# Pads between the memory pools of a two-block transformer kernel: moving operands 256 instead of 192 bytes behind the weights

## The chip, the cores and the metric

The kernel runs on 1 core of one Trainium2 chip. The metric is the device time of one execution in microseconds; three runs of the kernel before gave a median of 2269.2 us (2267.66 to 2282.68). Engines are named as in the profile: PE is TensorE's matmuls, PEld its weight loads, DVE is VectorE, ACT is ScalarE, POOL is GpSimd, SP is SyncE.

## What is computed

Two transformer stacks, one after the other, on 256 tokens of width 1024, all in float32:

```python
def first_block(x, ...):
    for i in range(DEPTH):                       # 4 layers
        m, j = i % N_MIXERS, i // N_MIXERS
        h = rms_norm(x, attn_norm[i])
        if m == 0:
            mix = diff_attention(h, a_w_qkv[j], ...)
        elif m == 1:
            mix = latent_attention(h, b_w_a[j], ...)
        else:
            mix = dilated_attention(h, c_w_qkv[j], ...)
        x = x + mix
        x = x + swiglu(rms_norm(x, ffn_norm[i]), f_w_gu[i], f_w_out[i])
    return rms_norm(x, final_norm)

def second_block(x, positions, ...):
    h = layer_norm(x, ln_in_g, ln_in_b)
    for l in range(DEPTH_2):                     # 2 layers
        mix = token_mix(h, ...)                  # pooling, causal convolution, sparse attention, gates
        h = layer_norm(DEEPNORM_ALPHA * h + mix, ln1_g[l], ln1_b[l])
        ffn = conv_ffn(h, w_up[l], ffn_dw_w[l], ffn_dw_b[l], w_down[l])
        h = layer_norm(DEEPNORM_ALPHA * h + ffn, ln2_g[l], ln2_b[l])
    return h
```

Nearly all the work is in projections of the form activations times weight matrix, with 256 tokens.

## The kernel before

**Three products for one.** Every float32 operand of a projection is split into a high and a low part of the type that TensorE takes at its fast rate (R, float32r). `weights` (L300) brings a weight tile from HBM into a tile "raw", ScalarE writes the high part "whi", VectorE or GpSimd the low part "wlo" (L313). `mm3` (L292) then issues three matmuls: whi with the high part of the activations, whi with the low part, wlo with the high part. All three lie on one line of the profile, L270 (`matmul`), and they are told apart there by their tiles.

**Two ways to project.** In `smode` and `smode2` (L330, L336) a 128x128 piece of the weights is the stationary operand and 256 tokens of activations are the moving operand. This is the form of the feed-forward layers (`ffn` L531, `conv_ffn` L1676), of `down` and of the output projections. In `mmode` (L353) a 128x128 piece of the activations is stationary and up to 512 columns of weights move; this is the form of the attention projections.

**Where operands lie.** Activations are either in the token block (tiles xh and xl, L388, 8 rows of 384 columns each) or in tiles "s" of the pool "big" (L262, four rows of 256 columns). Weights are in the pool "w" (raw, whi, wlo, tiles of up to 1024 columns, 4,096 bytes). The pools "const", "w", "big" and "wk" are laid out one behind the other in each partition's memory. Between them stand four tiles that nothing reads or writes, the pads: "padx" before xh, "padw" before the pool w, "padb" before big, "padk" before wk. Their widths in float32 columns are the tuple PADS (L32):

```python
PADS = (56, 72, 48, 80)
...
            pad = lambda n, cols: pool(n, 1).tile([128, cols], F32, name=n)
            pad("padw", PADS[1])
            self.wp = pool("w", 3)
            pad("padb", PADS[2])
            self.big = pool("big", 12)
            pad("padk", PADS[3])
            self.wk = pool("wk", 2)
```

In the built program all row lengths, tile sizes and steps of 128 weight columns of the large projections are multiples of 512 bytes, so the place of each operand, taken modulo 512, is the same for every row and tile of its pool: whi and wlo start at byte 75,968 and 100,544 (192 of 512), xh and xl at 25,472 and 37,760 (384), the tiles of big at 125,312 and multiples of 512 behind it (384). So in `smode` the moving operand lies 384 - 192 = 192 bytes of each 512 behind the weights, and in `mmode`, with the roles exchanged, 192 - 384 = 320 of 512. Two other places matter below: in `stacked_scores` (L650) stationary and moving operand both come from big, at a distance of 0 of 512; and the taps of the convolution (L1635) move `taps[:, n, d:d + 256]`, whose start goes up by 4 bytes with each tap d, high part (n = 0) from 384 of 512, low part (n = 1) 1,144 bytes behind it.

**Order.** TensorE's instructions stand in the order in which the program issues them, with a matmul's weight load ahead of it. Attention steps are woven into the projections by estimated times (`tick`, `later`), with a table of a matmul's duration by its columns (US, L29). Neither depends on the pads.

Of the kernel before, what the change touches and what calls it, by code (L numbers as in the profile page):

```python
# [28 lines left out]
US = {256: 0.12, 288: 0.132, 328: 0.155, 384: 0.175, 512: 0.235}  # L29
POOLED = (5, 7)  # L30
NH = 18
PADS = (56, 72, 48, 80)  # L32
WARM = 10
NORM, POOL = (7, 8, 9), 8
FILL = -3.0e38
# [177 lines left out]
class Program:  # L213
    def __init__(self, tc, ins, out, at):
# [3 lines left out]
        with ExitStack() as ctx:  # L218
            pool = lambda n, b, **k: ctx.enter_context(tc.tile_pool(name=n, bufs=b, **k))
            self.const = pool("const", 1)  # L220
# [7 lines that stand above are left out]
# [143 lines left out]
    def setup(self):  # L371
# [14 lines left out]
        self.ident = self.col("ident", 0, 128)  # L386
        c.tile([128, PADS[0]], F32, name="padx")
        self.xh = c.tile([128, 8, 384], R, name="xh")  # L388
# [1350 lines left out]
```

## Time and profile before

| | us |
|---|---|
| median of 3 runs | 2269.2 (2267.66 to 2282.68) |
| the profiled execution, its own time | 2279.07 |
| its span, first to last instruction | 2277.3 |
| TensorE matmuls busy | 2200.4 (97%) |
| VectorE busy | 1624.8 (71%) |
| ScalarE busy | 1325.4 (58%) |
| mean granted TensorE clock | 0.981 of full |

Matmul records overlap, since matmuls are pipelined: the record of one begins when it starts to read and its end is modelled. So the time that one costs in a dense stretch is the step from its start to the start of the next. In a table of stretches this comes out as the length of the stretch, plus the part of a record that hangs over, divided by the count.

### The profile page before, as it was taken

What the parts mean: (1) busy time and instruction counts of PE and PEld (TensorE: products, weight loads), DVE (VectorE), ACT (ScalarE), POOL (GpSimd) and SP (SyncE); (2) the same over time, 40 slices, a digit from 0 to 9 for tenths busy, and PEclk for the clock granted to TensorE, in tenths of its full rate; (3) what the DMA queues carried; (4) which work ended last, traced back from release to release, by engine and by line L of the source; (5) the groups of instructions that cost most, each with busy time, mean ns of one, the idle gap of its engine ahead of it and who ended that gap; (6) DMA issues with size and microseconds to landing.
All of it is one profiled execution on the core that took longest, in us unless ns stands there. A gap on an engine that the chain in (4) does not pass through costs nothing.

```text
span 2277.3 us, 42526 instructions
## 1 busy us (share of the span) xinstructions
PE 2200.4 (97%) x16676; PEld 2077.3 (91%) x16676; DVE 1624.8 (71%) x2940; ACT 1325.4 (58%) x2378; POOL 147.4 (6%) x169
## 2 busy tenths in 40 slices
PE   9999998999999999999999999989989998998998
PEld 7899997899978778999978999889989998998998
DVE  7776666776556656766577766796888789778875
ACT  7764457544556655644587545645567564656653
POOL 0000000100000000000000001110012011001211
PEclk9999999999999999999999999999989999998999
DMA  6345563355654334455633655544536544443653
GB/s 233 132 155 187 159 186 121 116 195 158 186 198 144 111 132 137 140 186 160 214 122 109 216 174 162 180 151 138 178 119 215 162 160 156 162 163 124 213 160 109
DMA packets 111801, 365.69 MB, mean 161 GB/s; under 512 B 12528, under 2 KB 14704, under 8 KB 111600
## 3 DMA queue, kind: packets, MB, share of 16 engines
q1 hardware_dynamic: 109728, 360.17, 48.1%
q10 hardware_dynamic: 1728, 2.54, 0.4%
q8 instruction: 131, 2.15, 0.4%
q14 instruction: 70, 0.57, 0.1%
q0 software_dynamic: 144, 0.26, 0.1%
HBM read 362.13 MB, written 1.05 MB: 159 GB/s over the span
## 4 chain that ended last, share of the span: by engine, by line
PE 72%; DVE 7%; ACT 4%; issue 1%; POOL 0%; ACTq 0%; DVEq 0%; POOLq 0%
PE mm L270 62%; PE sc L270 6%; PE tp L324 3%; DVE wlo L313 1%; ACT whi L241 1%; PE tp L270 1%; ACT xh L241 1%; ACT s L241 1%; ACT x L241 1%; PE tp L1141 0%; DVE score L1487 0%; DVE mx L1486 0%; PE tp L734 0%; DVE gut L244 0%; DVE acc L1130 0%
## 5 line engine op out<-in xcount | busy, mean ns | idle before, releaser
L313 DVE TENSOR_TENSOR wlo<-raw,whi 128x1024 fp32r<-128x1024 f32 (+3 forms) x752 | 844.7, 1127 | 337.4 <-ACT whi L241 334.0
L241 ACT ACTIVATE whi<-raw 128x1024 fp32r<-128x1024 f32 (+3 forms) x752 | 731.4, 978 | 559.8 <-PE mm L270 343.4
L270 PE MATMUL mm<-xh,wlo 128*128 128x256 f32 x2496 | 703.7, 282 | 16.7 <-DVE wlo L313 16.7
L270 PE MATMUL mm<-xh,whi 128*128 128x256 f32 x2496 | 710.3, 285 | 1.3 <-ACT whi L241 0.9
L270 PE MATMUL mm<-xl,whi 128*128 128x256 f32 x2496 | 703.6, 282 | 0.5 <-DVE xl L1191 0.5
L270 PE MATMUL mm<-s,whi 128*128 128x256 f32 x2944 | 524.4, 281 | 0.2 <-DVE s L244 0.2
L270 PEld LDWEIGHTS mm<-xh,wlo 128*128 128x128 f32 x2496 | 478.8, 192 | 17.6 <-DVE wlo L313 17.6
L270 PEld LDWEIGHTS mm<-xh,whi 128*128 128x128 f32 x2496 | 473.5, 190 | 3.8 <-ACT whi L241 1.3
L270 PEld LDWEIGHTS mm<-xl,whi 128*128 128x128 f32 x2496 | 475.1, 190 | 1.6 <-DVE xl L1191 0.9
L270 PEld LDWEIGHTS mm<-s,whi 128*128 128x128 f32 x2944 | 450.7, 188 | 2.6 <-issue 1.1
L270 PE MATMUL mm<-s,wlo 128*128 128x256 f32 x1472 | 412.3, 280 | 0.0
L270 PEld LDWEIGHTS mm<-s,wlo 128*128 128x128 f32 x1472 | 279.6, 190 | 0.0
L270 PE MATMUL mm<-whi,xh 128*128 128x512 f32 (+2 forms) x592 | 238.5, 404 | 8.2 <-ACT whi L241 4.4
L270 PE MATMUL mm<-wlo,xh 128*128 128x512 f32 (+2 forms) x592 | 233.2, 394 | 3.5 <-DVE wlo L313 3.5
L270 PE MATMUL mm<-whi,xl 128*128 128x512 f32 (+2 forms) x592 | 232.4, 393 | 0.0
L270 PEld LDWEIGHTS mm<-whi,xh 128*128 128x128 f32 x592 | 113.4, 192 | 29.9 <-ACT whi L241 5.0
L270 PEld LDWEIGHTS mm<-wlo,xh 128*128 128x128 f32 x592 | 113.7, 192 | 23.4 <-DVE wlo L313 4.8
L270 PEld LDWEIGHTS mm<-whi,xl 128*128 128x128 f32 x592 | 113.5, 192 | 22.0
L241 ACT ACTIVATE s<-guh 128x256 fp32r<-128x256 f32 x132 | 54.7, 415 | 103.8 <-DVE guh L558 93.3
L510 POOL TENSOR_TENSOR rstd<-ms,nhalf 128x2 f32<-128x2 f32 x29 | 30.0, 1034 | 1061.9 <-DVE ms L508 1053.5
L554 DVE TENSOR_TENSOR gut<-mm,rbc 128x512 f32<-128x512 f32 x88 | 60.4, 690 | 37.4 <-PE mm L270 37.2
L244 DVE SCALAR_TENSOR_TENSOR gut<-mm,pk,gut 128x255 f32<-128x255 f32 (+1 forms) x160 | 76.2, 478 | 7.2 <-ACT gut L241 5.0
(327 smaller groups left out, 2509.8 us busy)
## 6 DMA issues: line engine op xcount, KB each, us to landing
raw<-w_gu SPq DMA_DIRECT2D x176, 512.0 KB, 4.2
raw<-w_up SPq DMA_DIRECT2D x88, 512.0 KB, 4.3
raw<-w_zs SPq DMA_DIRECT2D x60, 512.0 KB, 4.7
raw<-w_out SPq DMA_DIRECT2D x64, 384.0 KB, 3.5
raw<-w_cqk SPq DMA_DIRECT2D x48, 512.0 KB, 4.2
raw<-w_out SPq DMA_DIRECT2D x64, 320.0 KB, 2.9
raw<-w_aqk SPq DMA_DIRECT2D x32, 512.0 KB, 4.8
raw<-w_cv SPq DMA_DIRECT2D x24, 512.0 KB, 3.6
```

The source lines that it names most:

```text
L241: return self.nc.scalar.activation(out, in_, func, bias=bias, scale=scale, **kw)
L244: return self.nc.vector.scalar_tensor_tensor(out, a, s, b, op0=op0, op1=op1)
L270: i = self.nc.tensor.matmul(*a, **kw)
L313: e.tensor_sub(lo, raw, hi.bitcast(F32))
L324: i = self.nc.tensor.transpose(out, in_, self.ident if ident is None else ident)
L510: self.powered = [self.nc.gpsimd.tensor_tensor(r, ms, self.nhalf[:, :n], op=OP.pow).ins]
L554: nc.vector.tensor_mul(t, ps, rb[:, None, :].to_broadcast([128, 2, 256]))
```

## The change

The widths of the four pads are set otherwise. Nothing else is changed.

```diff
-PADS = (56, 72, 48, 80)
+PADS = (72, 56, 64, 80)
```

"padx" grows by 16 columns (64 bytes) and "padw" shrinks by as much, so xh and xl move up by 64 bytes and the weights stay where they are. "padb" grows by 64 bytes, so big moves up by 64 bytes, and wk behind it too. In the built program:

| operand | byte before | of 512 | byte after | of 512 |
|---|---|---|---|---|
| xh | 25,472 | 384 | 25,536 | 448 |
| whi | 75,968 | 192 | 75,968 | 192 |
| tiles of big | 125,312 | 384 | 125,376 | 448 |
| first tile of wk | 174,784 | 192 | 174,848 | 256 |

So the moving operand of `smode` lies 448 - 192 = 256 bytes of each 512 behind the weights, and in `mmode` it is 192 - 448 = 256 of 512 as well. `stacked_scores` stays at 0. On every engine the same instructions stand in the same order as before, with the same waits.

## Rows read from the trace of the kernel before

**Rows 1.** The page: busy time by engine, and the chain's shares by line.

```profile
PE 2200.4 (97%) x16676; PEld 2077.3 (91%) x16676; DVE 1624.8 (71%) x2940; ACT 1325.4 (58%) x2378; POOL 147.4 (6%) x169
...
PE mm L270 62%; PE sc L270 6%; PE tp L324 3%; DVE wlo L313 1%; ACT whi L241 1%; PE tp L270 1%; ACT xh L241 1%; ACT s L241 1%; ACT x L241 1%; PE tp L1141 0%; DVE score L1487 0%; DVE mx L1486 0%; PE tp L734 0%; DVE gut L244 0%; DVE acc L1130 0%
```

**Rows 2.** Groups by form, PE: line, tiles, shape, count, busy us, mean ns, idle.

```profile
L270 PE MATMUL mm<-xh,whi 128*128 128x256 f32 x2464 | 700.3, 285 | 0.9 <-ACT whi L241 0.9
...
L270 PE MATMUL mm<-s,whi 128*128 128x256 f32 x2944 | 524.4, 281 | 0.2 <-DVE s L244 0.2
L270 PE MATMUL mm<-s,wlo 128*128 128x256 f32 x1472 | 412.3, 280 | 0.0
L270 PE MATMUL mm<-whi,xh 128*128 128x512 f32 x544 | 222.8, 411 | 8.2 <-ACT whi L241 4.4 <-ACT s L241 2.5 <-ACT qtok L241 1.1
```

**Rows 3.** Stretches: us, busy us (count) of PE, PEld, DVE, ACT, POOL, clock, DMA, GB/s.

```profile
152.00:302.00 150.00, 150.00 (x1276) 150.00 (x1275) 98.82 (x134) 72.91 (x109) 0.00 (x0) 1.00 0.56 177
449.00:599.00 150.00, 150.00 (x1276) 150.00 (x1276) 98.50 (x131) 72.25 (x106) 1.79 (x3) 1.00 0.59 187
949.00:1099.00 150.00, 150.00 (x1276) 150.00 (x1276) 98.89 (x134) 73.00 (x109) 0.00 (x0) 1.00 0.58 182
1262.00:1402.00 140.00, 140.00 (x1191) 140.00 (x1190) 92.58 (x124) 70.96 (x107) 2.75 (x3) 1.00 0.58 184
1409.00:1436.00 27.00, 27.00 (x232) 27.00 (x231) 25.06 (x37) 17.72 (x32) 9.60 (x10) 1.00 0.62 209
1696.00:1816.00 120.00, 120.00 (x1061) 120.00 (x1060) 98.03 (x154) 75.71 (x122) 17.84 (x15) 1.00 0.60 195
1822.00:1850.00 28.00, 28.00 (x240) 28.00 (x239) 25.07 (x39) 17.30 (x30) 6.77 (x7) 1.00 0.64 211
2006.00:2043.00 37.00, 37.00 (x328) 37.00 (x327) 30.46 (x62) 21.05 (x33) 0.00 (x0) 1.00 0.42 144
2105.00:2225.00 120.00, 120.00 (x1021) 120.00 (x1020) 94.96 (x147) 73.39 (x120) 19.09 (x15) 1.00 0.58 188
2236.00:2263.00 27.00, 27.00 (x241) 27.00 (x240) 17.00 (x28) 10.06 (x17) 6.27 (x7) 1.00 0.26 83
```

**Rows 4.** Groups by line in 152 to 302 us, then 1,696 to 1,816 us.

```profile
L270 PE MATMUL mm<-xh,wlo 128*128 128x256 f32 x314 | 88.2, 281 | 0.0
...
L270 PEld LDWEIGHTS mm<-xh,wlo 128*128 128x128 f32 x313 | 60.1, 192 | 0.0
L270 PEld LDWEIGHTS mm<-xl,whi 128*128 128x128 f32 x313 | 58.8, 188 | 0.0
...
L270 PE MATMUL mm<-xh,wlo 128*128 128x256 f32 x277 | 76.5, 276 | 0.0
...
L270 PEld LDWEIGHTS mm<-xh,wlo 128*128 128x128 f32 x276 | 51.8, 188 | 0.0
```

**Rows 5.** Timeline at 61.5 us (start, us, engine), then the loads' mean in ns.

```profile
61.78 1.60 PE L270 MATMUL sc<-s,s 128*128 128x256 f32 x12
...
L270 PEld LDWEIGHTS sc<-s,s 128*128 128x128 f32 x12 | 1.6, 191 | 0.1
```

**Rows 6.** Timeline of PE, taps 1, 11 and 13, and the matmul after tap 15.

```profile
1533.55 0.40 PE L270 MATMUL sc<-s,whi 128*128 128x256 f32 x2
...
1537.15 0.40 PE L270 MATMUL sc<-s,whi 128*128 128x256 f32 x2
...
1538.85 0.40 PE L270 MATMUL sc<-s,whi 128*128 128x256 f32 x2
...
1539.92 0.28 PE L270 MATMUL mm<-xh,whi 128*128 128x256 f32 x1
```

**Rows 7.** Timeline of PE in the first layer's query and key projection.

```profile
72.17 0.39 PE L270 MATMUL mm<-whi,xl 128*128 128x512 f32 x1
...
73.54 0.39 PE L270 MATMUL mm<-whi,xl 128*128 128x512 f32 x1
```

## Prediction, made before the result

> **What bounds the kernel now.** I read the page first (busy time and the chain that ended last), then the groups by line and form, then stretches by time, and last single rows of TensorE. TensorE is busy 97% of the span, and 62% of the chain is the one line that issues matmuls into the "mm" banks [rows 1]. So the end is set by how densely the matmuls follow each other, and nothing else in the change touches that: every engine keeps its instructions and their order, only addresses differ.
>
> Most of this work has one shape: 128x128 weights, 256 moving columns. There are three products for each pair, so 3 x 2,464 with the token block as moving operand (xh, xl), and 2,944 + 1,472 with tiles of the big pool ("s"): 11,808 matmuls [rows 2]. Their records are about 280 ns long but overlap; what counts is the step from one start to the next. In ten stretches the table shows TensorE filled without a hole, at the full clock (1.00, the level of 2.4 GHz), so the step is the window plus one record, over the count. In 152 to 302 us it is (150.00 + 0.28)/1,276 = 117.8 ns, and the same in two further stretches of that length; in 1,696 to 1,816 us it is (120.00 + 0.28)/1,061 = 113.4 ns [rows 3]. By this the ten stretches fall into two levels and nothing between: seven at 117 to 118 ns (1,276 + 1,276 + 1,276 + 1,191 + 232 + 240 + 1,021 = 6,512 matmuls in 765 us) and three at 113 to 114 ns (1,061 + 328 + 241 = 1,630 in 184 us). Both levels hold for hundreds of matmuls, with the same shapes, the same clock and the same 192 bytes of distance.
>
> The rows of one stretch of each kind show where they differ. At the upper level a matmul's record is 281 ns, and of the three weight loads of a triple one takes 192 ns and two take 188; at the lower level the records are 276 ns and every load takes 188 [rows 4]. So at the upper level a weight load is held up by something that recurs with the triple. VectorE and ScalarE do not explain it: they are busier in the lower-level stretch (98.03 and 75.71 of 120 us) than in the upper one (98.82 and 72.91 of 150 us) [rows 3]. What recurs with the triple is what TensorE itself reads: moving columns of one matmul while the next weights are loaded.
>
> The trace of before also has a few matmuls at other distances, since some operands lie differently. In the score products of the first layer weights and moving operand both come from the big pool, so their distance is 0 of 512. Twelve of them follow each other in (1.60 - 0.28)/11 = 120.0 ns, with loads of 191 ns on average: nearly every load is held up [rows 5]. And the taps of the convolution slide their moving operand by 4 bytes per tap (high part 192 + 4d bytes behind the weights, low part 312 + 4d). From tap 1 to tap 11 (196 to 236 bytes) 30 matmuls take 3.60 us, 120.0 ns each; in taps 13 to 15 (244 to 252 bytes) nine take 1.07 us, 118.9 ns each [rows 6].
>
> **The change part by part.** It removes and adds nothing. Moving operands in the token block and the big pool move up by 64 bytes, weights stay, so 192 becomes 256. Where the roles are exchanged (token block as weights, 512 weight columns moving) the distance goes from 320 to 256. The work pool moves by 64 bytes too, which leaves its distance to the big pool at 192 and touches only transposes and small products; I set those at nothing.
>
> The first term is the step of the 256-column matmuls at 256 bytes. No stretch of before has it with aligned rows, so it is bounded from both sides by the nearest rows. Below: the lower level, 113.4 ns, everywhere. The seven long stretches then give back 6,512 x (117.8 - 113.4) = 29 us. The matmuls outside the ten stretches are 11,808 - 8,142 = 3,666; with the same share of upper-level steps they would give another 13 us, so 42 us in all. Above: 120.0 ns everywhere, as at distance 0. The ten stretches hold 8,142 matmuls in 949 us; at 120.0 they take 977 us, 28 us more, and the others add 28 x 3,666/8,142 = 13 us: 41 us more.
>
> Between these ends I take the gain of the long stretches alone, 29 us, and nothing for the rest, because there the matmuls stand in short groups between other work. What leans to this side: 256 is the distance farthest from 0 both ways round, and 0 is where the rows show a load held up each time; and the taps get shorter, not longer, as they come near 256. It is a weak lean: the taps lie off the alignment of the big matmuls, their low part is elsewhere again, and 1.1 ns x 11,808 is only 13 us.
>
> The Trainium skill, page "TensorE: Matmul & The Clock Gate", section "Part 2: What happens when you issue a matmul", says that TensorE has two independent read ports, so that loading the next weights takes no read bandwidth from the running matmul. By that rule distance would do nothing and the sum would be 0; the 191 ns loads at distance 0 speak against it, the two levels at one distance for it [rows 4, 5].
>
> The second term is the 512-column matmuls, 3 x 544 [rows 2]. Their step is (73.54 - 72.17)/6 = 228 ns [rows 7], 7% over twice 106.7 ns, the 256 columns' own time at 2.4 GHz. With 3 ns either way, as between the levels above, 1,632 of them make 5 us up or down; I take 0.
>
> What hides a gain: nothing in the long gate and up stretches, where VectorE is busy two thirds to four fifths of the time and DMA 0.56 to 0.60 [rows 3]. In the stretch at 1,409 us VectorE has 25.06 of 27 us; at the lower level that work would fill it to 96%, so those 232 matmuls may keep a microsecond of their step. What is late next everywhere else is still TensorE.
>
> Sum: -29 us. The profiled execution took 2279.1 us (span 2277.3), which would become 2250; the three timed runs have a median of 2269.2 and reach from 2267.7 to 2282.7. The profiled one is thus near their upper end, which two long stretches at the other level would explain (1,276 x 4.4 ns = 5.6 us each). I set the sum against the median: 2240 us.
>
> **The rivals.**
> One, distance is not what decides, or 192 and 256 are alike. The level is then drawn anew after each stall: with all long stretches at the lower level it is 29 us less, with all at the upper one 1,630 x 4.4 ns = 7 us more, and as likely as not about the same number of each, so 2269 us. For it: both levels stand at one distance, and it changes from one stretch to another. Against it: distance 0 has a third, longer step.
>
> Two, it becomes slower: distance counts only within a shorter period than 512, of 128 or 256 bytes, because a weight load reads several parts of its 512 bytes side by side. Then 256 is the same as 0, each load is held up from the first matmul on, and no stretch reaches the lower level. The price is the upper end above, 28 to 41 us; I take 35, so 2304 us. It decides as soon as the parts are 256 bytes or shorter. For it: the step of 120.0 ns and the held-up loads at distance 0. Against it: the taps at 244 to 252 bytes don't get longer, though none of them lies exactly at 256 with aligned rows.
> The Trainium skill, same page, section "Weight-path perf modes", describes a weight load in four parallel chunks of 32 columns for types other than FP32; with 4 bytes per column that would be parts of 128 bytes, and the sum would be that of this rival. The trace cannot say whether it applies to these loads.
>
> **How the numbers follow.** A measurement here tells about 1% (23 us) from no change. Forecast 0.38, first rival 0.31, second rival 0.31. The forecast lies over the line of 1%, most of the first rival within it, the second over it on the other side. So faster 0.38, same 0.31, slower 0.31. The forecast's own range is 2225 (42 us, and a little) to 2252. The whole range has to reach over the other cases: from 2222 to 2308, with the far ends of either mechanism left out.
>
> **What would show it.** In the stretch from 152 us on, 150 us would hold 1,326 matmuls at the lower level, 1,276 if nothing changes, 1,252 at 120 ns. Right: records of 276 ns and loads of 188 in all gate and up stretches, no load group at 192. Wrong by the first rival: again stretches of both kinds, perhaps others than now. Wrong by the second: all loads at 191 to 192, and no stretch under 120 ns. A step under 113 ns, or over 120, would mean that neither of my bounds holds.

## The result, and the profile after

The changed kernel takes 2300.8 us (median; single runs 2298.8 to 2302.7), the kernel before 2268.4 us on the same chip (2267.3 to 2282.7): the ratio is 1.0132, with a 95% interval from 1.0105 to 1.0158. It became slower, by 32 us. The prediction of 2240 us was wrong in its sign; the measured time lies within its whole range, close to the second rival's 2304 us.

The page's line of busy times, of the changed kernel (that of before: [rows 1]):

```profile
PE 2227.5 (97%) x16676; PEld 2108.2 (92%) x16676; DVE 1626.9 (71%) x2940; ACT 1324.9 (58%) x2378; POOL 150.5 (7%) x169
```

Only TensorE's two rows have grown by more than 3 us (27 and 31); VectorE, ScalarE and GpSimd do the same work in nearly the same time. The stretches of [rows 3], after the change (columns as there: us, busy us and count of PE, PEld, DVE, ACT and POOL, granted clock, DMA share, GB/s):

```profile
152.00:302.00 150.00, 150.00 (x1252) 150.00 (x1251) 96.86 (x131) 71.06 (x108) 0.00 (x0) 1.00 0.54 173
...
1262.00:1402.00 140.00, 140.00 (x1170) 140.00 (x1170) 94.91 (x125) 68.45 (x101) 2.29 (x2) 1.00 0.57 186
...
1696.00:1816.00 120.00, 116.77 (x959) 116.36 (x958) 99.69 (x161) 77.92 (x133) 23.31 (x18) 0.99 0.53 176
1822.00:1850.00 28.00, 28.00 (x233) 27.85 (x232) 20.21 (x35) 13.24 (x22) 3.58 (x4) 1.00 0.46 140
```

The first shows 1,252 matmuls where before it was 1,276: (150.00 + 0.28)/1,252 = 120.0 ns. The two levels of before (117.8 and 113.4 ns) are both gone. (Later windows no longer begin at the same place of the program, since the work in front of them takes longer; the third has a gap at its start, the fourth the end of the stretch.) The groups by line in 152 to 302 us, to be held against the first half of [rows 4]:

```profile
L270 PE MATMUL mm<-xh,wlo 128*128 128x256 f32 x312 | 88.3, 283 | 0.0
...
L270 PEld LDWEIGHTS mm<-xh,whi 128*128 128x128 f32 x311 | 59.7, 192 | 0.0
L270 PEld LDWEIGHTS mm<-xl,whi 128*128 128x128 f32 x311 | 59.7, 192 | 0.0
L270 PEld LDWEIGHTS mm<-xh,wlo 128*128 128x128 f32 x311 | 59.7, 192 | 0.0
```

Now every one of the three loads of a triple takes 192 ns, where before one took 192 and two 188. The groups by form, against [rows 2]:

```profile
L270 PE MATMUL mm<-xh,whi 128*128 128x256 f32 x2464 | 707.1, 287 | 0.2
...
L270 PE MATMUL mm<-s,whi 128*128 128x256 f32 x2944 | 538.2, 284 | 0.0
L270 PE MATMUL mm<-s,wlo 128*128 128x256 f32 x1472 | 416.9, 283 | 0.0
L270 PE MATMUL mm<-whi,xh 128*128 128x512 f32 x544 | 221.0, 407 | 8.0 <-ACT whi L241 4.2 <-ACT s L241 2.5 <-ACT qtok L241 1.1
```

Where the time came from: I took, of all 256-column matmuls of the two groups, the differences of consecutive starts that are 130 ns or less (11,491 of them before, 11,505 after), and from here on a "step" is such a difference. Its mean goes from 116.8 to 119.9 ns; over 11,808 matmuls that is 37 us more. The same for the 512-column matmuls gives 229.8 before and 228.4 ns after, 2 us less over 1,632. That is 35 us more, where the profiled spans differ by 23.5 (2277.3 and 2300.8). Most of what lies between is the granted clock: its mean in the profiled execution is 0.981 before and 0.987 after, so by an estimate before lost 0.019 x 2277 = 43 us of full-speed time and after 0.013 x 2301 = 30 us. That the pads moved the clock is not shown: timed executions of the kernel before have means from 0.981 to 0.988. The timed medians are 32 us apart, near the 35.

### The profile page after: what moved, and what is told of

Its sections match the earlier page's. It is cut to its first block, busy times and chain, and to the rows that moved or that the text cites. A ratio compares the mean times of both kernels' runs of the same rounds, so it can differ in the third digit from the quotient of the medians.

```text
span 2300.8 us, 42526 instructions
## 1 busy us (share of the span) xinstructions
PE 2227.5 (97%) x16676; PEld 2108.2 (92%) x16676; DVE 1626.9 (71%) x2940; ACT 1324.9 (58%) x2378; POOL 150.5 (7%) x169
## 4 chain that ended last, share of the span: by engine, by line
PE 73%; DVE 6%; ACT 4%; issue 1%; POOL 0%; ACTq 0%; DVEq 0%; POOLq 0%
PE mm L270 63%; PE sc L270 6%; PE tp L324 2%; DVE wlo L313 1%; ACT whi L241 1%; PE tp L270 1%; ACT xh L241 1%; ACT x L241 1%; ACT s L241 0%; DVE score L1487 0%; PE tp L1141 0%; PE tp L734 0%; DVE mx L1486 0%; DVE gut L244 0%; DVE acc L1130 0%
## 5 line engine op out<-in xcount | busy, mean ns | idle before, releaser
L270 PE MATMUL mm<-s,whi 128*128 128x256 f32 x2944 | 538.2, 284 | 0.0
L270 PEld LDWEIGHTS mm<-xh,whi 128*128 128x128 f32 x2496 | 482.6, 193 | 2.6 <-issue 1.0
L270 PEld LDWEIGHTS mm<-xl,whi 128*128 128x128 f32 x2496 | 482.8, 193 | 1.5 <-DVE xl L1191 0.9
L270 PEld LDWEIGHTS mm<-s,whi 128*128 128x128 f32 x2944 | 460.4, 192 | 2.1 <-issue 1.1
L270 PEld LDWEIGHTS mm<-wlo,xh 128*128 128x128 f32 x592 | 113.3, 191 | 22.6 <-DVE wlo L313 4.8
```

The costliest lines, as they stand in the source:

```text
L270: i = self.nc.tensor.matmul(*a, **kw)
```

## The experiments

In all kernels of the first seven runs only the four pads differ, so every engine has the same instructions in the same order. Two distances can be set apart: that of the token block to the weights (7,392 matmuls of 256 columns) and that of the big pool's tiles (4,416). My theories: (P) the distance counts with a period of 128 bytes (distances that differ by 128 act alike), (H) with a period of 256, (W) with a period of 512 and 256 a bad value in it, (A) not the distance counts but the place of the moving block. Each kernel's ratio is to the kernel before, timed on the same chip. The two windows shown of each run lie in the gate and up groups of the first layer (160 to 250 us, token block) and in its down projection (275 to 315 us, big pool). Before, they hold 767 and 342 matmuls, 117.7 and 117.8 ns each:

```profile
160.00:250.00 90.00, 90.00 (x767) 90.00 (x766) 62.39 (x82) 43.54 (x64) 0.00 (x0) 1.00 0.55 181
275.00:315.00 40.00, 40.00 (x342) 40.00 (x341) 23.13 (x32) 18.36 (x27) 0.00 (x0) 1.00 0.61 180
```

**Distance or place.** The weights come down to 128 of 512, the moving blocks stay at 384.

```diff
-PADS = (56, 72, 48, 80)
+PADS = (56, 56, 64, 80)
```

> The pads (56, 56, 64, 80): the moving blocks of both groups of products stay at 384 of 512 bytes, where they lay before the change, and the weights come down to 128 of 512 in their place, so that the distance is 256, as after the change. If the distance decides (by either period), the kernel is as after the change: every long stretch at 120.0 ns, 1,252 matmuls in a window of 150 us, 2295 to 2305 us. If the place of the moving block in 512 bytes decides, it is as before the change: stretches at about 113.4 and 117.8 ns, 1,270 matmuls or more in such a window, 2262 to 2285 us.

2303.0 us, ratio 1.0150 (1.0112 to 1.0188).

```profile
160.00:250.00 90.00, 90.00 (x752) 90.00 (x751) 61.08 (x80) 43.02 (x64) 0.00 (x0) 1.00 0.56 176
275.00:315.00 40.00, 40.00 (x336) 40.00 (x335) 23.15 (x33) 18.26 (x26) 0.00 (x0) 1.00 0.64 181
```

(90 + 0.28)/752 and (40 + 0.28)/336 are 120.0 and 119.9 ns. The moving operands lie where they lay before, and the kernel is as after the change, where it was the weights that kept their place: what the two have in common is the distance. (A) falls.

**One part alone.** Only the token block goes to 256.

```diff
-PADS = (56, 72, 48, 80)
+PADS = (72, 56, 48, 80)
```

> The pads (72, 56, 48, 80): only the token block's moving operands (7,392 of the 11,808 matmuls of 256 columns of the two groups) lie 256 behind their weights, the other 4,416 stay at 192. If the distance sets each matmul's step by itself, the token block's stretches stand at 120.0 ns and the others at 113.4 or 117.8 ns; the time is between: 7,392 x 3.2 ns = 24 us over the kernel before, 2285 to 2298 us. If a stretch's level is drawn once for the whole run and the distance only shifts the draw, both groups move together: all at 120.0 (about 2300 us) or none (about 2269 us).

2283.6 us, ratio 1.0060 (1.0040 to 1.0079), a little under the expected band.

```profile
160.00:250.00 90.00, 90.00 (x752) 90.00 (x751) 61.04 (x80) 43.19 (x64) 0.00 (x0) 1.00 0.55 176
275.00:315.00 40.00, 40.00 (x355) 40.00 (x354) 23.11 (x34) 19.29 (x28) 0.00 (x0) 1.00 0.67 188
```

The token block stands at 120.0 ns: the distance acts on each group by itself. But the other group, whose distance of 192 was not touched, went from 117.8 to 40.28/355 = 113.5 ns. Over the run 86% of its steps are now 113 or 114 ns, where it was 26% before. That gives back (116.6 - 114.0) x 4,416 = 11 us of the 3.0 x 7,392 = 22 us that the token block loses. This was not expected by any theory; the last runs go after it.

**64 and 128.**

```diff
-PADS = (56, 72, 48, 80)
+PADS = (40, 104, 32, 80)
```

> The pads (40, 104, 32, 80): token block at a distance of 64, the other group at 128. If the period is 128 bytes, 64 is as 192 (steps of 113.4 or 117.8 ns) and 128 is as 256 (120.0 ns): 4,416 x 3.2 ns = 14 us over the kernel before, 2275 to 2290 us. If the period is 256 bytes and only 0 of it is bad, both are fast: 2260 to 2285 us with no stretch at 120.0. If it is 512 bytes with 256 alone special, nothing forbids a third level at either distance.

2275.9 us, ratio 1.0038 (1.0017 to 1.0058): within the bands of both periods. The traces tell them apart: at 64 the two levels of before, at 128 no level at all, only 45% of the steps at 119 to 121 ns (table below). (P) falls.

```profile
160.00:250.00 90.00, 90.00 (x767) 90.00 (x766) 62.39 (x82) 43.56 (x64) 0.00 (x0) 1.00 0.57 181
275.00:315.00 40.00, 40.00 (x339) 40.00 (x338) 22.89 (x33) 18.56 (x27) 0.00 (x0) 1.00 0.63 177
```

In the second window a matmul at 128 takes 40.28/339 = 118.8 ns.

**224 and 160.**

```diff
-PADS = (56, 72, 48, 80)
+PADS = (56, 64, 40, 80)
```

> The pads (56, 64, 40, 80): token block at a distance of 224, the other group at 160, neither a multiple of 64. If what counts is how far the distance is from a multiple of 128, both lie between the good 192 and the bad 256 or 128, and the steps lie between 113.4 and 120.0 ns: 2265 to 2290 us. If what counts is that the two are not multiples of 64 bytes, so that no draw between two levels is left, both groups stand at one level: 113.4 ns throughout would be 11,808 x (116.8 - 113.4) = 40 us under the kernel before, 2225 to 2240 us; 117.8 throughout would be 12 us over it, 2275 to 2285 us.

2290.0 us, ratio 1.0087 (1.0053 to 1.0122), the upper end of the first band. Neither group has a level; the means are 118.3 (token) and 117.8 ns. That no level is left off the multiples of 64 held; that both groups would then stand at one step throughout did not.

**320 and 0.**

```diff
-PADS = (56, 72, 48, 80)
+PADS = (72, 40, 0, 80)
```

> The pads (72, 40, 0, 80): token block at a distance of 320, the other group at 0. So far 256 gave 120.0 ns at nearly every step, 64 and 192 two levels (113.4 and 117.8 ns), 128 scattered steps with a mean of 118.6 to 119.0. If the rule has a period of 256 bytes, 320 is as 64 (two levels) and 0 is as 256 (120.0 ns): the group at 0 then costs 4,435 x 3.2 ns = 14 us over the kernel before, 2275 to 2292 us. If 256 alone of the 512 bytes is special (the far end), 0 is another value than 120.0: either a longer step, if the load and the moving block then meet in the same bank at the same time (130 ns or more would be 60 us over), or a shorter one (113.4 throughout: 15 us under, 2255 us).

2296.1 us, ratio 1.0115 (1.0072 to 1.0159), 4 us above the band of the period of 256. Its windows:

```profile
160.00:250.00 90.00, 90.00 (x766) 90.00 (x766) 62.23 (x81) 43.55 (x64) 0.00 (x0) 1.00 0.56 180
275.00:315.00 40.00, 40.00 (x336) 40.00 (x335) 22.72 (x32) 17.86 (x25) 0.00 (x0) 1.00 0.61 178
```

Distance 0 is 40.28/336 = 119.9 ns, the same as 256. What I had left out is the 512-column matmuls, which with the roles exchanged lie at 192 here: 233.3 ns against 229.8, 6 us over 1,632 of them; and the token block at 320 had only 1% of its steps at the lower level.

**96 and 32.**

```diff
-PADS = (56, 72, 48, 80)
+PADS = (72, 96, 8, 80)
```

> The pads (72, 96, 8, 80): token block at a distance of 96, the other group at 32, the last two distances of the first 256 bytes. With 160 and 224 (means 117.8 and 118.3 ns, spread over 115 to 124) as the pattern of distances that are no multiple of 64, both groups stand at a mean of 117.5 to 118.5 ns with no long stretch at one step: 11,800 x (118 - 116.8) = 14 us over the kernel before, 2278 to 2295 us. If instead the rule is the distance from 256 in one direction alone, 96 and 32 are better than 192: a mean under 116 ns and a time under 2260 us.

2297.8 us, ratio 1.0126 (1.0090 to 1.0163), 3 us above the first band. The token block at 96 is worse than I expected (120.0 ns on average), the other group at 32 better (117.0), and the 512-column matmuls are the slowest of all, 234.0 ns.

**448 and 384.**

```diff
-PADS = (56, 72, 48, 80)
+PADS = (72, 8, 96, 80)
```

> The pads (72, 8, 96, 80): token block at a distance of 448, the other group at 384, which a period of 256 makes equal to 192 and 128. By that period: the token block at 113.4 and 117.8 ns in long stretches, the other group scattered with a mean of 118.6 to 119.0: 2272 to 2290 us. If the period is 512: values of their own; a group that stands at 113.4 throughout would be seen by 1,320 matmuls in a window of 150 us.

2281.1 us, ratio 1.0043 (1.0022 to 1.0064). No stretch stands at one level of its own, so nothing here asks for a period of 512. The steps by distance in seven of these kernels, from the starts in their traces:

```text
distance  group, kernel            steps  mean ns   at 113-114  117-118  119-121  other
  0       big, (320, 0)            4,305   119.9         0%        2%      96%      1%
256       big, after               4,303   119.9         0%        3%      97%      1%
256       token, after             7,202   119.9         0%        2%      97%      0%
 64       token, (64, 128)         7,200   116.5        28%       64%       8%      0%
192       token, before            7,190   116.9        20%       70%       9%      1%
192       big, before              4,301   116.6        26%       65%       8%      1%
320       token, (320, 0)          7,195   117.7         1%       88%      11%      0%
448       token, (448, 384)        7,185   115.7        48%       46%       6%      1%
128       big, (64, 128)           4,303   118.7         0%       21%      45%     34%
384       big, (448, 384)          4,303   119.4         0%       27%      39%     33%
 32       big, (96, 32)            4,303   117.0        16%       28%      28%     28%
 96       token, (96, 32)          7,211   120.0         0%       22%      21%     56%
160       big, (224, 160)          4,303   117.8         0%       33%      36%     31%
224       token, (224, 160)        7,206   118.3         0%       30%      17%     53%
```

0 and 256 are one kind: 120 ns at nearly every step. 64, 192, 320 and 448 are one kind: two levels, in shares that differ from kernel to kernel. 128 and 384 are a third, scattered over 115 to 124 ns, and the four odd multiples of 32 scatter as well. That is a period of 256 bytes (H); by (P) 128 would have been as 256. At none of the twelve distances tried is the lower level the only one. The 512-column matmuls have their own order: 228.4 ns at 256, 229.8 at 64 and 320, 233 to 234 at 192, 448, 288 and 416.

**What picks the level at 192.** In the trace of before I looked at the unbroken runs of at least 12 steps, 69 of them. From their fourth step on, 30 are at the lower level to their end and 39 at the upper; the level changes only where another shape or a wait interrupts. And in the run with the token block alone, all six long stretches at 192 that followed straight on a stretch at 256 stood at the lower level. So a level may be a phase between the moving reads and the weight loads that each step hands to the next, and a few matmuls at 256 ahead of a stretch might set it. They are extra work: their sums are overwritten by the group behind them. AT is the first of the weight columns that they use: 112 columns are 448 bytes, which puts these weights at 128 of 512, 256 behind which the moving block lies.

```diff
+STEER, AT = 12, 112
...
+        for _ in range(STEER if steer else 0):
+            self.matmul(ps[:, 0, :], w(0, AT)[0], xs[0][0], start=True, stop=True, skip_group_check=True)
         for k in range(n):
...
-        return self.smode2(self.weights(self.ins["w_gu"][l, j], 256), xs)
+        return self.smode2(self.weights(self.ins["w_gu"][l, j], 256), xs, steer=j == 3)
...
```

> The pads of before (distance 192). At 8 places, ahead of one group in each long stretch (4 of the feed-forward layers at j = 3, 2 of the token mixing at j = 7, 2 of the convolving feed-forward at j = 4), 12 more matmuls of 256 columns, whose weights are columns 112 to 239 of the same tile, so that their moving operand lies 256 behind them; what they write is overwritten by the group. In the run with the token block alone at 256, all six stretches at 192 that followed a stretch at 256 without a gap came out at the lower level (113.4 ns). If a stretch's level is set by the phase with which it is entered, and a distance of 256 sets that phase, all long stretches behind the 12 stand at 113.4: about 9,000 matmuls x (117.7 - 113.4) x the part that was at the higher level (about 3/4) = 29 us under, 8 x 12 x 0.120 = 12 us over: 2245 to 2260 us, and 1,318 matmuls or more in most windows of 150 us. If the six were chance, the levels are drawn as before and the time is 12 us above it: 2275 to 2290 us.

The control, with AT = 0:

> The control to the run before: the same 12 more matmuls at the same 8 places, but with columns 0 to 127 of the tile as weights, so that their distance is 192 like that of the group itself. They can't change the phase: levels drawn as in the kernel before, 12 us over it, 2275 to 2290 us. If it is not the distance but the extra work at the place that helps, this one comes out like its twin.

2279.3 us, ratio 1.0032 (1.0014 to 1.0049), and 2278.9 us, ratio 1.0024 (0.9998 to 1.0049): as slow as each other, and no gain. Both are 5 us over before rather than 12. Two of the eight places, in the convolving layers, lie ahead of a wait of 3.1 us, which shrinks to 1.7 in the first of the two runs, so the 12 cost nothing there; that is 3 of the 7 us, and the rest is not accounted for. In the first run the 12 stand at 120 ns from the second to the eleventh, and behind them the stretch is at the upper level again, in all four feed-forward layers:

```profile
158.00:308.00 150.00, 150.00 (x1276) 150.00 (x1275) 95.90 (x128) 70.76 (x104) 0.00 (x0) 1.00 0.56 176
458.00:608.00 150.00, 150.00 (x1276) 150.00 (x1276) 94.60 (x124) 69.03 (x99) 0.00 (x0) 1.00 0.56 176
958.00:1108.00 150.00, 150.00 (x1276) 150.00 (x1275) 95.97 (x128) 70.80 (x104) 0.00 (x0) 1.00 0.56 176
1272.00:1402.00 130.00, 130.00 (x1106) 130.00 (x1106) 84.91 (x114) 62.71 (x95) 1.75 (x2) 1.00 0.55 175
```

So a distance of 256 does not by itself lead to the lower level. What was different in the run with the token block alone: there the moving block steps back by 64 bytes where the distance goes from 256 to 192; here the weights step forward by 64 (modulo 512).

```diff
-            self.matmul(ps[:, 0, :], w(0, AT)[0], xs[0][0], start=True, stop=True, skip_group_check=True)
+            self.matmul(ps[:, 0, :], w(0, 0)[0], self.xh[:, 0, 16:272], start=True, stop=True, skip_group_check=True)
...
+        nc.vector.tensor_copy(self.xh[:, 0, 256:272], self.ident[:, :16])
```

> As the run with 12 matmuls at 256 and shifted weights, but here the weights stay (columns 0 to 127) and the moving operand is shifted: columns 16 to 271 of the token block's first chunk, 64 bytes higher, so that it is the moving block that steps back by 64 bytes as the distance goes from 256 to 192, as in the run with the token block alone at 256. If what sets the lower level is that step of the moving block, the stretches behind the 12 stand at 113.4 ns: 2245 to 2262 us, windows of 150 us with 1,318 matmuls or more. If the lower level there came from something else (the group of the feed-forward's second half, its weights), they stay at 117.7 as in the shifted-weights run: 2272 to 2290 us.

2254.2 us, ratio 0.9915 (0.9885 to 0.9945). The stretches behind the 12, in the four feed-forward layers, with (150 + 0.28)/1,326 and (130 + 0.28)/1,150, both 113.3 ns:

```profile
158.00:308.00 150.00, 150.00 (x1326) 150.00 (x1325) 99.14 (x134) 73.92 (x108) 0.00 (x0) 1.00 0.60 181
449.00:599.00 150.00, 150.00 (x1326) 150.00 (x1325) 98.31 (x130) 71.44 (x104) 0.00 (x0) 1.00 0.62 187
943.00:1093.00 150.00, 150.00 (x1326) 150.00 (x1325) 100.52 (x137) 73.62 (x111) 0.00 (x0) 1.00 0.60 184
1252.00:1382.00 130.00, 130.00 (x1150) 130.00 (x1149) 87.40 (x116) 65.05 (x98) 2.77 (x3) 1.00 0.60 182
```

Two kernels, alike in distances, counts and places of the extra work, differ in which operand steps by 64 bytes (modulo 512), and all four feed-forward layers are at the upper level in the one and at the lower in the other. In the convolving layers the extra work stood ahead of a wait of 2 us, and what it set was lost.

Then with STEER = 4 and with 2, without the places in the token mixing, and in the convolving layers four groups later (j = 8):

> The run with 12 matmuls of shifted moving operand, cut to 4 and to the six long stretches (the four feed-forward layers at j = 3, the two convolving ones at j = 8, behind their slow start): 6 x 4 matmuls, 6 x 4 x 0.120 = 3 us, where 8 x 12 cost 11.5. In the run with 12 the step stood at 120 from the third of them on, so 4 should do. If so all six stretches, about 8,000 matmuls, stand at 113.4: 2254 less 8.6 less about 2.5 for the stretch at 1683 that then stood at 117.7 = 2243 us, range 2235 to 2250; windows of 150 us with 1,320 to 1,326 matmuls. If 4 do not bring the phase over, levels as drawn before: 2268 to 2282 us.

> The same with 2 instead of 4. In the run with 12 the first of them took 113 and the second 119 ns before the step stood at 120, so with 2 the phase is not yet at its resting place when the distance goes back to 192. If the phase must have rested, the stretches come out at either level, 2245 to 2282 us, not all six alike; if the step back by 64 bytes is enough, all six stand at 113.4 and the time is 1.4 us under the run with 4.

2257.1 us, ratio 0.9949 (0.9929 to 0.9969), and 2254.4 us, ratio 0.9951 (0.9927 to 0.9976): less gain than expected with 4, about the expected with 2. In both runs the four feed-forward layers, entered at the upper level, go to the lower. The convolving stretches that were entered at the lower level, both with 4 and one with 2, fell to the upper; the one entered at the upper rose. In the three that fell the steps at 256 were 119, 113, 116 and 119 ns with 4, and 119 and 113 with 2: not yet at rest when the distance went back. So "4 should do" held only for stretches entered at the upper level. One of those that fell, with 4 (start, us, engine; x5 is the 4 and the group's own first matmul):

```profile
1687.76 0.28 PE L271 MATMUL mm<-xl,whi 128*128 128x256 f32 x1
...
1688.33 0.75 PE L271 MATMUL mm<-xh,whi 128*128 128x256 f32 x5
1688.92 0.28 PE L271 MATMUL mm<-xl,whi 128*128 128x256 f32 x1
...
1689.98 0.28 PE L271 MATMUL mm<-xl,whi 128*128 128x256 f32 x1
```

Ahead of the 4, five steps take 1688.33 - 1687.76 = 0.57 us, 114 ns each; behind them, nine take 1689.98 - 1688.92 = 1.06 us, 118 ns each.

The last run gives 2 to the feed-forward layers and 12 to the convolving ones:

```diff
...
-        return self.smode2(self.weights(self.ins["w_gu"][l, j], 256), xs)
+        return self.smode2(self.weights(self.ins["w_gu"][l, j], 256), xs, steer=2 if j == 3 else 0)
...
-                ps = self.smode2(self.weights(up[l, j], 256), xs)
+                ps = self.smode2(self.weights(up[l, j], 256), xs, steer=12 if j == 8 else 0)
```

> 2 of the shifted matmuls in the four feed-forward layers, which every profiled run entered at the higher level, and 12 in the two convolving ones, which are entered at either level. With 4 or 2 there, the step had not come to rest at 120 when a stretch entered at 113.4 went back to 192, and it fell to 117.7 (three of three). If a rest at 256 followed by a step back of the moving block leads to the lower level whatever the level before, both convolving stretches stand at 113.4 behind the 12: all six long stretches at 113.4, 2246 to 2256 us. If the level before carries through, a stretch entered at 113.4 comes out at 117.7 again: 2250 to 2262 us.

2252.4 us, ratio 0.9929 (0.9902 to 0.9956). Its stretches, all six:

```profile
168.00:318.00 150.00, 150.00 (x1326) 150.00 (x1325) 97.43 (x132) 74.03 (x108) 0.00 (x0) 1.00 0.61 183
447.00:597.00 150.00, 150.00 (x1326) 150.00 (x1326) 99.59 (x133) 72.72 (x107) 0.00 (x0) 1.00 0.62 190
941.00:1091.00 150.00, 150.00 (x1326) 150.00 (x1325) 100.47 (x137) 74.18 (x110) 0.00 (x0) 1.00 0.60 185
1248.00:1378.00 130.00, 130.00 (x1150) 130.00 (x1149) 89.25 (x120) 66.84 (x101) 2.78 (x3) 1.00 0.60 185
1690.00:1785.00 95.00, 95.00 (x841) 95.00 (x840) 76.70 (x124) 60.53 (x98) 15.06 (x12) 1.00 0.58 179
2103.00:2198.00 95.00, 95.00 (x840) 95.00 (x839) 75.78 (x119) 60.07 (x98) 14.36 (x11) 1.00 0.56 177
```

95.28/841 is 113.3 ns too. Both convolving stretches were entered at the lower level, as with 4, and keep it behind 12. The timeline at the first of them (start, us, engine; a row with x13 is the 12 and the group's own first matmul):

```profile
1685.51 0.28 PE L270 MATMUL mm<-xh,wlo 128*128 128x256 f32 x1
1685.62 1.71 PE L270 MATMUL mm<-xh,whi 128*128 128x256 f32 x13
1687.16 0.28 PE L270 MATMUL mm<-xl,whi 128*128 128x256 f32 x1
...
1688.19 0.28 PE L270 MATMUL mm<-xl,whi 128*128 128x256 f32 x1
```

The 13 take 1687.16 - 1685.62 = 1.54 us, 118.5 ns each; after them nine steps take 1.03 us, 114 ns each. The groups of the stretch from 168 us on show what the lower level is, [rows 4] with the long loads gone:

```profile
L270 PE MATMUL mm<-xl,whi 128*128 128x256 f32 x266 | 73.4, 276 | 0.0
...
L270 PEld LDWEIGHTS mm<-xh,whi 128*128 128x128 f32 x265 | 49.7, 188 | 0.0
```

This version beats both kernels: 16 us under the kernel before, with the pads of before and 32 matmuls more (4 x 2 and 2 x 12, 4 us by 0.120 each).

## Why the prediction was wrong

**What bounds the kernel** was right: TensorE's step sets the end. 37 us more of steps went with 32 us more of time, and no other engine's busy time moved by more than 3 us.

**The first term failed**, at the sentence "Between these ends I take the gain of the long stretches alone, 29 us". It forecast 29 us less, and the steps of the 256-column matmuls took 37 us more. The bounds of the step were right (113.4 and 120.0 ns; after has 119.9), the choice between them was not. Of the two reasons given, "256 is the distance farthest from 0 both ways round" assumed a period of 512 bytes. The runs show one of 256, in which 256 is 0: 119.9 ns at both, with 96 to 97% of the steps at 119 to 121. The score products at distance 0 [rows 5] were thus the exact precedent, 120.0 ns and loads of 191, and I set them at the far end. The second reason, "the taps get shorter, not longer, as they come near 256", rested on nine matmuls at distances that are no multiple of 32 and whose low part lies elsewhere; I called it weak, at 13 us, and still let it pick the sign.

**The second term** (512 columns) was taken at 0 within 5 us: it measured -1.4 ns each, 2 us less. Its bound of 3 ns, taken "as between the levels above" where those lie 4.4 apart, was too narrow in general: the same matmuls take 3.3 to 4.2 ns more at 192, 448, 288 and 416.

**The first rival** (levels drawn anew) is wrong for 256, where only one level exists, but describes 64, 192, 320 and 448 in part: a level is kept until an interruption. It isn't an even draw. In the seven profiled kernels that enter the feed-forward stretches at 192 behind the same short interruption (tile tp, L324), all 28 entries are at the upper level. The runs also hint at where the spread of times comes from: the two kernels with only 120 ns in both groups (after, and the run with the weights moved) each lie within 4.3 us in four executions, the kernel before between 2256 and 2283 us, in many more executions and on several chips. That the levels differ between executions was not shown directly, since each kernel has one profile.

**The second rival** was right in what it showed and in its price: 1,252 matmuls in 152 to 302 us as it said, all loads at 192, no long stretch below 119.9 ns, and +32 us where it had 28 to 41, taken at 35. The price itself was worked out a little too high: 949 us leaves out the record that hangs over each of the ten windows (0.28 us), so 120.0 ns would be 25 us more there and 11 outside, 36 in all; the steps gave 37. Its condition was parts "of 128 or 256 bytes"; 256 is what the runs leave. Its reason, that a load reads parts of its 512 bytes side by side, is not shown: the runs show the period, not what makes it. The four chunks of 32 columns that the Trainium skill describes (page "TensorE: Matmul & The Clock Gate", section "Weight-path perf modes") would, by my estimate at 4 bytes a column, make a period of 128 bytes. The runs don't show that: distances 128 and 384 (118.7 and 119.4 ns, scattered) don't behave as 0 and 256 do. The same page of the Trainium skill says in "Part 2: What happens when you issue a matmul" that loading the next weights doesn't steal read bandwidth from the running matmul. The runs disagree for these operands: with nothing changed but addresses, step and load depend on how far apart the two reads lie, by up to 6.7 ns per matmul (113.3 and 120.0). What the two share is not shown.

**Two levels at one distance** I had read rightly as something that recurs with the triple, but had no cause for. The runs with extra matmuls show that it is history: the same code, addresses and neighbours stand at 113.3 or 117.8 ns by how the stretch was entered. The forecast's mechanism, all long stretches at 113.4, thus exists, and the last run has it in its six long stretches, but at a distance of 192. Profile against profile it gives 27 us (spans of 2277.3 and 2250.0), about the 29 less the 4 that the 32 extra matmuls cost; 25 of 100 steps in the down groups and 16 in the token groups are still above the lower level. Median against median it is 16 us, because the profiled execution of before, on which the 29 rested, took 11 us more than the median (2279.1 against 2268.4 us), and the forecast set its gain against the median.

Still open: why a rest at 256 ends in the lower level when the moving block steps back and in the upper one when the weights step forward, and whether a 16-byte offset would do better; neither was tried further.

## What to carry to other kernels

Where matmuls follow each other without a gap and weight loads run beside them, measure the step from start to start, and look at where moving operand and weights lie to each other modulo 256 bytes: with 256 columns, 64 and 192 gave 115.7 to 117.7 ns on average here, and a multiple of 256 gave 120 at nearly every step (96 came to 120 on average too). With 512 columns 256 was best. An exact precedent in the trace, even of twelve instructions, is worth more than a trend from rows that lie off the alignment; before taking a distance as "far", ask with which period it counts. And where one kernel shows two levels with the same addresses, look at what entered the stretch: two cheap matmuls ahead of 1,440 others were worth (117.8 - 113.3) x 1,440 = 6 us in each of three layers.

## What the runs showed of the hardware that was not expected

- The step of a 128x128, 256-column matmul at the full clock (1.00) depends on the distance between moving operand and next weights with a period of 256 bytes: 119.9 ns at 0 and 256; 113.3 or 117.8 at 64, 192, 320 and 448; scattered with a mean of 117.0 to 120.0 at the other multiples of 32 that were tried.
- At 64, 192, 320 and 448 the level lasts until another shape or a wait interrupts it. From the fourth step on, that holds for all 69 unbroken runs of at least 12 steps in the trace of before, and for all 47, 46 and 50 of the token block at 64, 320 and 448.
- A few matmuls at 256, with the moving block 64 bytes higher, ahead of a stretch at 192 bring it to the lower level: 17 of 17 stretches entered at the upper level (feed-forward layers: four with 12, four with 4, eight with 2; one convolving stretch with 2), two of two entered at the lower level with 12, none of three with 4 or 2. With the weights 64 bytes lower (modulo 512) instead, four of four stayed at the upper level.
- The 512-column matmul has its best distance at 256 (228.4 ns), where the 256-column one stands at 119.9 at nearly every step.
